# Dense projections of a two-layer encoder by token: activations stationary, 512 weight columns moving

## The chip, the cores and the metric

The kernel runs on one core of one Trainium2 chip. The metric is device time in microseconds (us) of a whole execution, median of three runs. A span in the profile runs from the first to the last instruction of one profiled execution and is a little shorter.

## The reference, cut to what matters

One sequence of 256 tokens, model width 1024, two layers, all in float32. Each layer does this (FFN width 2816, 8 query heads and 2 key heads of 64, conv width 512 with 31 taps):

```python
h = x + 0.5 * swiglu(rms_norm(x, norm_ffn1[i]), w_ffn1_in[i], w_ffn1_out[i])
u = rms_norm(h, norm_mix[i])
q, k, v, c, g = jnp.split(u @ w_in[i], splits, axis=-1)
y_attn = window_attention(q, k, v, sink[i], rel_bias) @ w_attn_out[i]
c_val, c_gate = jnp.split(c, 2, axis=-1)
c = depthwise_conv(c_val * jax.nn.sigmoid(c_gate), conv_w[i], conv_b[i])
y_conv = jax.nn.silu(layer_norm(c, conv_ln_g[i], conv_ln_b[i])) @ w_conv_out[i]
g_attn, g_conv = jnp.split(jax.nn.sigmoid(g), 2, axis=-1)
h = h + (g_attn * y_attn + g_conv * y_conv) @ w_o[i]
h = h + 0.5 * swiglu(rms_norm(h, norm_ffn2[i]), w_ffn2_in[i], w_ffn2_out[i])
x = h + (p[i] @ w_pe_proj[i]) * jax.nn.sigmoid(rms_norm(h, norm_pe[i]) @ w_pe_gate[i])
```

## The kernel before

Weights are 200 MB and are read once, in the order of use, through SyncE's queue into four 1 MB tiles called `raw`. To keep float32 accuracy, class `Weights` splits each block in two: ScalarE (ACT) casts `raw` to float32r as `w_hi` (L100), and VectorE (DVE) subtracts to get `w_lo` (L101); seven such pairs are in flight. Activations are split in the same way (`x0h`, `x0l`, `h_hi`, `h_lo`), and a product is three matmuls, high by high, high by low and low by high (`mm3`, L311 to L313).

Before, the 128x128 weight block is the stationary operand and the 256 tokens move: a matmul yields 128 features by 256 tokens in PSUM. So everything is held features on partitions: the residual `x32`, the SwiGLU layer `h`, the gates `g`. A norm's mean square is summed by GpSimd (POOL) and turned into a row that all partitions hold by a matmul with ones (`ps_stat`, L409). Only keys, values and queries (`ps_kv`, `ps_q`, L664 to L710) are made with the activation stationary. The two branch outputs `attn_out` (`ps_ao`) and `conv_out` (`ps_co`, both L837) use the raw float32 weights with no split; such a matmul leaves two records in the trace.

Each layer goes: FFN in (`ps_gu`), FFN out (`ps_fo`), then `mix`, then a second FFN, then `embed` (`ps_pp`, `ps_pe`). Inside `mix` TensorE computes conv input `ps_c`, keys, values, queries, scores `ps_s`, transposes `ps_pt`, `ps_o` and gates `ps_g`; meanwhile DVE does the convolution, 31 taps for each of four channel blocks on tile `y` (L600). Then come `ps_ao` with the conv layer norm between (mean `ps_mu` L856, variance `ps_var` L866, then `rs`, SiLU), then `ps_co`, then `ps_wo`.

A table of relative positions, `tb`, is made during the first FFN, written 128 times to DRAM as `tb_d` (2 MB from 8 partitions, L526) and read back skewed as `bias` (L530). Both transfers are issued by ACT's queue, which stands still until the first has landed before it issues the second.

A scheduler puts each engine's instructions in program order with priorities; each engine then works strictly in that order. The convolution taps have a background priority, so they fill what DVE has left.

Of the kernel before, what the change touches and what calls it, by code (L numbers as in the profile page):

```python
# [15 lines left out]
P = 128  # L16
T = 256
D = 1024
KD = D // P
L = 2  # L20
# [12 lines left out]
NEG = -1e9  # L33
LOOK = 6
# [4 lines left out]
W_BUFS = 7  # L39


class Weights:
# [16 lines left out]
    def spec(self, k, n, pieces):  # L59
        """pieces: (unit, first k of the unit, first column of the unit, first column here, columns)."""  # L60
        self.specs.append((k, n, pieces, False))

    def raw_spec(self, unit, k, c0, n):
        self.specs.append((k, n, [(unit, 0, c0, 0, n)], True))

    def limit(self):
        held = [p[0] for s in self.specs[self.next_get : self.next_prep] if s[3] for p in s[2]]
        return min(held) + RAW_BUFS - 1 if held else len(self.units) - 1

    def load_upto(self, u):  # L70
        while self.next_load <= min(u, self.limit(), len(self.units) - 1):
            k, n, sources = self.units[self.next_load]
            t = self.raw_pool.tile([P, KD * 256], F32, name="raw", tag="raw")
            v = t[:, : k * n].rearrange("p (k n) -> p k n", n=n)
            for place, src in sources:
                self.nc.sync.dma_start(place(v), src)
            self.raw[self.next_load] = v
            self.next_load += 1

    def prep_upto(self, i):  # L80
        nc = self.nc
        while self.next_prep <= min(i, len(self.specs) - 1):
            k, n, pieces, as_is = self.specs[self.next_prep]
            for u, *_ in pieces:
                self.load_upto(u + RAW_BUFS - 2)
                if u >= self.next_load:
                    return
            if as_is:
                ((u, k0, s0, _, w),) = pieces
                self.ready[self.next_prep] = self.raw[u][:, k0 : k0 + k, s0 : s0 + w]  # L90
                self.next_prep += 1
                continue
            hi = self.w_pool.tile([P, KD * P], F32R, name="w_hi")
            lo = self.w_pool.tile([P, KD * P], F32R, name="w_lo")
# [44 lines left out]
def encoder_kernel(ctx: ExitStack, tc: tile.TileContext, a: dict, out: bass.AP):  # L139
# [9 lines left out]
    mmp = ctx.enter_context(tc.tile_pool(name="mmp", bufs=4, space=PS))  # L149
    atp = ctx.enter_context(tc.tile_pool(name="atp", bufs=2, space=PS))  # L150

    def mm_tile(name):
        return mmp.tile([P, 512], F32, name=name, tag="mm")

    def at_tile(name):
        return atp.tile([P, 1024], F32, name=name, tag="at")

    # ---------------------------------------------------------------- inputs
# [3 lines left out]
    x_ld = raw_pool.tile([P, 2, D], F32, name="x_ld", tag="raw")  # L162
    xv = a["x"][0].rearrange("(t p) d -> p t d", p=P)
    for i in range(4):
        s = slice(i * 256, (i + 1) * 256)
        nc.sync.dma_start(x_ld[:, :, s], xv[:, :, s])

    col = {}
    par = const.tile([P, 96], F32, name="par")
# [13 lines left out]
    def place_params(tile_, rows, c0):  # L183
        r0 = 0
        for name in rows:
            n = 1 if name in ("q_norm", "k_norm") else a[name].shape[1] // P
            col[name] = (c0 + r0, n)
            r0 += L * n
        ps = at_tile("ps_par")
        nc.tensor.transpose(ps[:, :r0], tile_[:r0, :], ident[:r0, :r0])  # L190
        nc.scalar.copy(out=par[:, c0 : c0 + r0], in_=ps[:, :r0])
        return c0 + r0

    rows_first = const.tile([L * KD, P], F32, name="rows_first")
    load_params(rows_first, ("norm_ffn1",), nc.scalar.dma_start)

    # --------------------------------------------------------- weight stream
# [5 lines left out]
    def cols_unit(w, k, c0, n):  # L203
        return ws.unit(k, n, [(whole, w[: k * P, c0 : c0 + n].rearrange("(k p) n -> p k n", p=P))])

    def ffn_specs(w_in, w_out, quick=False):
        for j in range(KF // 2):
            if quick and j == 0:
                for c in range(2):
                    for c0 in (0, FF):  # L210
                        u = cols_unit(w_in, KD, c0 + c * P, P)
                        ws.spec(KD, P, [(u, 0, 0, 0, P)])
                continue
            ug = cols_unit(w_in, KD, j * 256, 256)
            uu = cols_unit(w_in, KD, FF + j * 256, 256)
            for c in range(2):
                ws.spec(KD, P, [(ug, 0, c * P, 0, P)])
                ws.spec(KD, P, [(uu, 0, c * P, 0, P)])
        for f in range(KD // 2):
            us = [  # L220
                ws.unit(n, 256, [(whole, w_out[k0 * P : (k0 + n) * P, f * 256 : (f + 1) * 256].rearrange("(k p) n -> p k n", p=P))])
                for k0, n in KGROUPS
            ]
            for c in range(2):
                for u, (_, n) in zip(us, KGROUPS):
                    ws.spec(n, P, [(u, 0, c * P, 0, P)])

    KGROUPS = [(0, 8), (8, 7), (15, 7)]

    def mix_specs(l):  # L230
        w = a["w_in"][l]
        c0 = QD + 2 * P

        def conv_specs(j, n):
            uv = cols_unit(w, KD, c0 + j * P, n * P)
            ug = cols_unit(w, KD, c0 + CD + j * P, n * P)
            for c in range(n):
                ws.spec(KD, P, [(uv, 0, c * P, 0, P)])
                ws.spec(KD, P, [(ug, 0, c * P, 0, P)])

        conv_specs(0, 2)
        ukv = cols_unit(w, KD, QD, 256)
        for i in range(2):
            ws.spec(KC, 256, [(ukv, i * KC, 0, 0, 256)])
        for i in range(2):
            uq = cols_unit(w[i * KC * P : (i + 1) * KC * P], KC, 0, QD)
            for k in range(0, KC, 2):
                ws.spec(2, QD, [(uq, k, 0, 0, QD)])
        conv_specs(2, 2)
        g0 = QD + 2 * P + 2 * CD  # L250
        for j in range(8):
            u = cols_unit(w, KD, g0 + j * 256, 256)
            for c in range(2):
                ws.spec(KD, P, [(u, 0, c * P, 0, P)])
        w = a["w_attn_out"][l]
        for j in range(2):
            src = w[:, j * 512 : (j + 1) * 512].rearrange("(v c p) n -> v p c n", v=2, p=HD)
            u = ws.unit(KC, 512, [
# [3 lines left out]
            for c in range(2):  # L262
                ws.raw_spec(u, KC, c * 256, 256)
        w = a["w_conv_out"][l]
        for j in range(2):
            u = cols_unit(w, KC, j * 512, 512)
            for c in range(2):
                ws.raw_spec(u, KC, c * 256, 256)
        w = a["w_o"][l]
        for j in range(4):  # L270
            u = cols_unit(w, KD, j * 256, 256)
            for c in range(2):
                ws.spec(KD, P, [(u, 0, c * P, 0, P)])

    def pe_specs(l):
        up = cols_unit(a["w_pe_proj"][l], 2, 0, 1024)
        for c in range(2):
            ws.spec(2, 512, [(up, 0, c * 512, 0, 512)])
        for j in range(4):
            u = cols_unit(a["w_pe_gate"][l], KD, j * 256, 256)  # L280
            for c in range(2):
                ws.spec(KD, P, [(u, 0, c * P, 0, P)])
# [7 lines left out]
    # ------------------------------------------------------------- constants  # L290
    ones_d = const.tile([P, P], F32, name="ones_d")
    nc.gpsimd.memset(ones_d, 1.0 / D)
# [11 lines left out]
    # -------------------------------------------------------------- helpers  # L304
    def mm3(ps, w, x, first=True, last=True, k0=0, x_k0=0, n_k=None, cols=slice(0, P)):
        (wh, wl), (xh, xl) = w, x
        n_k = wh.shape[1] if n_k is None else n_k
        for k in range(n_k):
            kx = x_k0 + k
            f, e = first and k == 0, last and k == n_k - 1  # L310
            nc.tensor.matmul(ps, wh[:, k0 + k, cols], xh[:, kx, :], start=f, stop=False)  # L311
            nc.tensor.matmul(ps, wh[:, k0 + k, cols], xl[:, kx, :], start=False, stop=False)  # L312
            nc.tensor.matmul(ps, wl[:, k0 + k, cols], xh[:, kx, :], start=False, stop=e)  # L313

    def pair(name, x, fresh):
        """Two products with x in one PSUM tile [P, 2, T]; right behind the evacuation that
        made x (fresh) its last block comes last."""
        if not fresh:
            ps = mm_tile(name).rearrange("p (c t) -> p c t", c=2)
            return ps, [lambda c=c: mm3(ps[:, c, :], ws.get(), x) for c in range(2)]  # L320
# [745 lines left out]
```

## Time and profile before

| what | value |
|---|---|
| device time, median of 3 | 1199.72 us (1199.09 to 1199.82) |
| span of the profiled execution | 1195.8 us; its own time was not kept apart, so the 3.9 us to the median stand for what lies around the span |
| TensorE (PE) matmul busy | 1160.1 us, 97% |
| DVE busy | 812.5 us, 68% |
| ACT busy | 613.9 us, 51% |
| POOL busy | 89.4 us, 7% |
| weights read by SyncE's queue | 200.01 MB |

PE waits in few places: the start, about 19 us in the first FFN, and a few us in each `mix`. In the chain of work that ended last, PE holds 91% and the transfer into `tb_d` 4%.

### The profile page before, as it was taken

How to read it: one execution, taken by the hardware profiler on the slowest of the kernel's cores; microseconds unless marked ns; L12 is line 12 of the kernel's file. 1: busy time of each engine (PE TensorE's matmuls, PEld its weight loads, DVE VectorE, ACT ScalarE, POOL GpSimd, SP SyncE). 2: the span in 40 equal slices, each digit the busy share in tenths (PEclk: the TensorE clock that was granted, in tenths of full speed). 3: DMA queues.
4: the chain of work that ended last, by engine and by line, in shares of the span. 5: the costliest groups of instructions: out<-in, count | busy, mean ns of one | idle time of the engine just before them, and what ended most of it. 6: DMA issues, size and time to landing. Idle time of an engine off the chain costs nothing.

```text
span 1195.8 us, 21809 instructions
## 1 busy us (share of the span) xinstructions
PE 1160.1 (97%) x9082; PEld 1125.0 (94%) x9082; DVE 812.5 (68%) x1214; ACT 613.9 (51%) x1033; POOL 89.4 (7%) x119
## 2 busy tenths in 40 slices
PE   7985999999999999999999999999999999999998
PEld 7985999999789999999999999999978899999997
DVE  5825765699767766665786666568986786666564
ACT  6614444477535544444674444447753564444443
POOL 3000001130001000000010000112100020000110
PEclk9996999999999999999999999999999999999999
DMA  8957645656136664555656555565531665644541
GB/s 248 288 99 209 229 151 173 215 179 152 59 105 205 193 211 158 188 180 175 200 162 210 169 179 163 194 212 177 142 106 36 213 220 175 199 154 159 194 142 36
DMA packets 196710, 205.07 MB, mean 171 GB/s; under 512 B 3731, under 2 KB 188899, under 8 KB 196612
## 3 DMA queue, kind: packets, MB, share of 16 engines
q1 hardware_dynamic: 194508, 200.01, 52.4%
q10 hardware_dynamic: 2104, 3.68, 1.9%
q8 instruction: 71, 1.16, 0.4%
q14 instruction: 27, 0.22, 0.1%
HBM read 200.53 MB, written 3.15 MB: 170 GB/s over the span
## 4 chain that ended last, share of the span: by engine, by line
PE 91%; DMA 5%; DVE 2%; ACT 1%; issue 0%; ACTq 0%
PE ps_gu L313 13%; PE ps_gu L311 13%; PE ps_gu L312 13%; PE ps_fo L312 7%; PE ps_fo L313 7%; PE ps_fo L311 7%; DMA tb_d<-tb 4%; PE ps_g L311 3%; PE ps_g L313 3%; PE ps_g L312 3%; PE ps_co L837 2%; PE ps_s L745 1%; PE ps_c L311 1%; PE ps_pe L313 1%; PE ps_pe L311 1%; PE ps_pe L312 1%
## 5 line engine op out<-in xcount | busy, mean ns | idle before, releaser
L101 DVE TENSOR_TENSOR w_lo<-raw,w_hi 128x1024 fp32r<-128x1024 f32 (+1 forms) x368 | 440.9, 1202 | 266.8 <-ACT w_hi L100 264.3
L100 ACT CAST w_hi<-raw 128x1024 fp32r<-128x1024 f32 (+1 forms) x368 | 377.4, 1030 | 443.2 <-PE ps_gu L312 196.7
L312 PE MATMUL ps_fo<-h_lo,w_hi 128*128 128x256 f32 x704 | 198.9, 283 | 0.0
L313 PE MATMUL ps_fo<-h_hi,w_lo 128*128 128x256 f32 x704 | 198.9, 283 | 0.0
L311 PE MATMUL ps_fo<-h_hi,w_hi 128*128 128x256 f32 x704 | 198.9, 283 | 0.0
L312 PEld LDWEIGHTS ps_fo<-h_lo,w_hi 128*128 128x128 f32 x704 | 135.1, 192 | 0.0
L311 PEld LDWEIGHTS ps_fo<-h_hi,w_hi 128*128 128x128 f32 x704 | 135.1, 192 | 0.0
L313 PEld LDWEIGHTS ps_fo<-h_hi,w_lo 128*128 128x128 f32 x704 | 135.1, 192 | 0.0
L400 POOL TENSOR_TENSOR sq_acc<-sq_acc,sq 128x256 f32<-128x256 f32 x56 | 56.3, 1005 | 924.7 <-ACT sq L399 924.2
L311 PE MATMUL ps_gu<-x0h,w_hi 128*128 128x256 f32 x352 | 102.6, 291 | 19.6 <-ACT w_hi L100 17.4
L313 PE MATMUL ps_gu<-x0h,w_lo 128*128 128x256 f32 x352 | 102.2, 290 | 0.7 <-DVE w_lo L101 0.7
L312 PE MATMUL ps_gu<-x0l,w_hi 128*128 128x256 f32 x352 | 101.8, 289 | 0.0
L600 DVE SCALAR_TENSOR_TENSOR y<-cpad,cw,y 128x256 f32<-128x256 f32 x240 | 101.1, 476 | 0.1
L312 PE MATMUL ps_gu<-xf1l,w_hi 128*128 128x256 f32 x352 | 100.0, 284 | 0.0
L311 PE MATMUL ps_gu<-xn0h,w_hi 128*128 128x256 f32 x352 | 100.0, 284 | 0.0
L312 PE MATMUL ps_gu<-xf0l,w_hi 128*128 128x256 f32 x352 | 99.9, 284 | 0.0
L311 PE MATMUL ps_gu<-xf1h,w_hi 128*128 128x256 f32 x352 | 99.9, 284 | 0.0
L311 PE MATMUL ps_gu<-xf0h,w_hi 128*128 128x256 f32 x352 | 99.8, 284 | 0.0
L313 PE MATMUL ps_gu<-xn0h,w_lo 128*128 128x256 f32 x352 | 99.8, 284 | 0.0
L313 PE MATMUL ps_gu<-xf1h,w_lo 128*128 128x256 f32 x352 | 99.8, 283 | 0.0
L313 PE MATMUL ps_gu<-xf0h,w_lo 128*128 128x256 f32 x352 | 99.8, 283 | 0.0
L312 PE MATMUL ps_gu<-xn0l,w_hi 128*128 128x256 f32 x352 | 99.8, 283 | 0.0
(222 smaller groups left out, 2727.9 us busy)
## 6 DMA issues: line engine op xcount, KB each, us to landing
raw<-in_w_ffn_in_dram SPq DMA_DIRECT2D x86, 1024.0 KB
raw<-in_w_in_dram SPq DMA_DIRECT2D x30, 1024.0 KB
raw<-in_w_ffn_out_dram SPq DMA_DIRECT2D x32, 896.0 KB
raw<-in_w_ffn_out_dram SPq DMA_DIRECT2D x16, 1024.0 KB
raw<-in_w_o_dram SPq DMA_DIRECT2D x8, 1024.0 KB
raw<-in_w_pe_gate_dram SPq DMA_DIRECT2D x8, 1024.0 KB
raw<-in_w_attn_out_dram SPq DMA_DIRECT2D x8, 512.0 KB
raw<-in_w_conv_out_dram SPq DMA_DIRECT2D x4, 1024.0 KB
```

Source lines behind the costliest of these rows:

```text
L100: nc.scalar.copy(out=hv[:, :, d0 : d0 + w], in_=src),
L101: nc.vector.tensor_tensor(out=lv[:, :, d0 : d0 + w], in0=src, in1=hv[:, :, d0 : d0 + w].bitcast(F32), op=ALU.subtract,),
L311: nc.tensor.matmul(ps, wh[:, k0 + k, cols], xh[:, kx, :], start=f, stop=False)
L312: nc.tensor.matmul(ps, wh[:, k0 + k, cols], xl[:, kx, :], start=False, stop=False)
L313: nc.tensor.matmul(ps, wl[:, k0 + k, cols], xh[:, kx, :], start=False, stop=e)
L400: nc.gpsimd.tensor_tensor(out=self.acc, in0=self.acc, in1=sq, op=ALU.add)
L600: nc.vector.scalar_tensor_tensor(out=y[:, i, :], in0=src, scalar=w, in1=y[:, i, :], op0=ALU.mult, op1=ALU.add)
L745: nc.tensor.matmul(ps[:, c, :], qT[v * HD : (v + 1) * HD, c, qb * P : (qb + 1) * P], kT[v * HD : (v + 1) * HD, :], start=True, stop=True,)
L837: nc.tensor.matmul(ps[:, c * T : (c + 1) * T], w[:, k, c * P : (c + 1) * P], x[:, k, :], start=k == 0, stop=k == KC - 1,)
```

## The change

It turns the dense projections around. The activation's 128 tokens by 128 features are stationary (two token blocks, `NT`), and 512 weight columns move; a matmul yields 128 tokens by 512 features (`mm3`, new L294 to L296). The function `chunk` does a whole product for 512 columns in two PSUM banks; the weight pieces change shape but not size. The residual is now `x_tok`, tokens on partitions. So a norm's gain becomes a row multiplied on DVE, its mean square an ACT accumulation, and its factor `r_x` a scalar for each partition, applied in the evacuation; no `ps_stat` any more. But the next product needs features on partitions, so each such operand goes back through PE transposes: `turn` (`ps_x`) after each norm and for the gated sum `ym`, `ps_h` for the inner layer of the FFN, `ps_ct` for the convolution's input. The final transposes of the output go away. `attn_out` and `conv_out` now use split weights and 512 columns, two chunks each in place of four pieces. Layer-norm work is now in pieces of 512 columns. The two transfers `tb_d` and `bias` are issued by POOL's queue (new L451, L455), and the gains of later norms are loaded through that queue too.

```diff
-    def mm3(ps, w, x, first=True, last=True, k0=0, x_k0=0, n_k=None, cols=slice(0, P)):
...
-            nc.tensor.matmul(ps, wh[:, k0 + k, cols], xh[:, kx, :], start=f, stop=False)
-            nc.tensor.matmul(ps, wh[:, k0 + k, cols], xl[:, kx, :], start=False, stop=False)
-            nc.tensor.matmul(ps, wl[:, k0 + k, cols], xh[:, kx, :], start=False, stop=e)
+    def mm3(ps, x, kx, t, w, k, first, last):
+        (xh, xl), (wh, wl) = x, w
+        xh, xl = xh[:, kx, tok(t)], xl[:, kx, tok(t)]
+        nc.tensor.matmul(ps, xh, wh[:, k, :], start=first, stop=False)
+        nc.tensor.matmul(ps, xh, wl[:, k, :], start=False, stop=False)
+        nc.tensor.matmul(ps, xl, wh[:, k, :], start=False, stop=last)
...
+    def turn(x, k0, t, src):
+        ps = tr_tile("ps_x").rearrange("p (f q) -> p f q", q=P)
+        for f in range(4):
+            nc.tensor.transpose(ps[:, f, :], src[:, f * P : (f + 1) * P], ident)
+        split([h[:, k0 : k0 + 4, tok(t)] for h in x], ps)
...
+        def scale(self, t, c):
+            xg = tmp.tile([P, N], F32, name="xg", tag="row", bufs=3)
+            nc.vector.tensor_tensor(out=xg, in0=x_tok[:, t, cols(c)], in1=self.gain[:, cols(c)], op=ALU.mult)
+            junk = tmp.tile([P, N], F32, name="sqj", tag="row", bufs=3)
+            nc.scalar.activation(
+                out=junk, in_=x_tok[:, t, cols(c)], func=AF.Square, scale=D ** -0.5,
+                accum_out=self.ss[:, t, c : c + 1],
+            )
+            return lambda: turn(self.x, c * KC, t, xg)
...
-        nc.scalar.dma_start(tb_d.rearrange("q h m -> h q m"), tb.unsqueeze(1).broadcast_to([NH, P, NREL]))
+        nc.gpsimd.dma_start(tb_d.rearrange("q h m -> h q m"), tb.unsqueeze(1).broadcast_to([NH, P, NREL]))
...
-        nc.scalar.dma_start(bias, skew)
+        nc.gpsimd.dma_start(bias, skew)
...
+                def turn_h():
+                    ps = tr_tile("ps_h").rearrange("p (f t) -> p f t", f=2)
+                    for f in range(2):
+                        for t in range(NT):
+                            nc.tensor.transpose(ps[:, f, tok(t)], hh[:, t, f * P : (f + 1) * P], ident)
+                    split([p[:, 2 * j : 2 * j + 2, :] for p in h], ps)
+
+                ws.later(2, turn_h)
...
-            for i in range(KC):
-                if i == 1:
-                    ln_mean()
-                if i == 2:
-                    ln_scale()
-                attn_out(2 * i)
-                if i == 0:
-                    squash(12)
...
+            attn_out(0)
+            squash(0)
+            squash(2)
+            ln_mean()
+            ws.later(2, ln_scale)
+            attn_out(1)
...
+            for c in range(2):
+                acc = acc_tile("ps_co")
+                chunk(acc, KC, yp, 2 if c else 0, after=lambda t: urgent(t, 1, acc))
```

Three places in the order of instructions matter below. The first is PE in layer 1 at the conv layer norm. Before, the last gate products are followed by `ps_ao` in four pieces with the norm's matmuls spread between them:

```order
L311 MATMUL ps_g<-xm0h,w_hi 128x256
L312 MATMUL ps_g<-xm0l,w_hi 128x256
L313 MATMUL ps_g<-xm0h,w_lo 128x256
L837 MATMUL ps_ao<-o,raw 128x256 x8
L856 MATMUL ps_mu<-y,ones_c 128x256 x2
L837 MATMUL ps_ao<-o,raw 128x256 x6
L856 MATMUL ps_mu<-y,ones_c 128x256
L837 MATMUL ps_ao<-o,raw 128x256 x2
L856 MATMUL ps_mu<-y,ones_c 128x256
L866 MATMUL ps_var<-ysq,ones_c 128x256 x2
L837 MATMUL ps_ao<-o,raw 128x256 x9
```

After, on PE at the same place, from the end of the second and last `ps_ao` chunk:

```order
L294 MATMUL ps_ao<-w_hi,o_h 128x512
L295 MATMUL ps_ao<-w_lo,o_h 128x512
L296 MATMUL ps_ao<-w_hi,o_l 128x512
L784 MATMUL ps_mu<-y,ones_c 128x256 x2
L794 MATMUL ps_var<-ysq,ones_c 128x256 x4
L294 MATMUL ps_co<-w_hi,y_h 128x512
L295 MATMUL ps_co<-w_lo,y_h 128x512
```

The second half of the mean and all of the variance now stand behind the last `ps_ao` matmul, with `ps_co` next, which needs the norm's result.

The second place is DVE at the same stage. Before, from the last gates to the norm's end:

```order
L818 TENSOR_TENSOR g<-ps_g,r_x 128x512
L600 SCALAR_TENSOR_TENSOR y<-cpad,cw,y 128x256 x12
L818 TENSOR_TENSOR g<-ps_g,r_x 128x512
L600 SCALAR_TENSOR_TENSOR y<-cpad,cw,y 128x256 x6
L847 TENSOR_TENSOR g<-ps_ao,g 128x512
L600 SCALAR_TENSOR_TENSOR y<-cpad,cw,y 128x256 x2
L847 TENSOR_TENSOR g<-ps_ao,g 128x512
L858 TENSOR_TENSOR y<-y,ps_mu 128x512 x2
L101 TENSOR_TENSOR w_lo<-raw,w_hi 128x1024 x2
L847 TENSOR_TENSOR g<-ps_ao,g 128x512
L366 RECIPROCAL rs<-sd 128x256
L870 TENSOR_TENSOR y<-y,rs 128x256 x4
```

After, on DVE, from the evacuation of the first `ps_ao` chunk (L767; taps are L538, weight splits L89):

```order
L767 TENSOR_TENSOR g<-ps_ao,g 128x512 x2
L538 SCALAR_TENSOR_TENSOR y<-cpad,cw,y 128x256 x4
L89 TENSOR_TENSOR w_lo<-raw,w_hi 128x1024
L538 SCALAR_TENSOR_TENSOR y<-cpad,cw,y 128x256 x2
L89 TENSOR_TENSOR w_lo<-raw,w_hi 128x1024
L767 TENSOR_TENSOR g<-ps_ao,g 128x512 x2
L538 SCALAR_TENSOR_TENSOR y<-cpad,cw,y 128x256
L89 TENSOR_TENSOR w_lo<-raw,w_hi 128x1024
L538 SCALAR_TENSOR_TENSOR y<-cpad,cw,y 128x256 x10
L786 TENSOR_TENSOR y<-y,ps_mu 128x512 x2
L798 RECIPROCAL rs<-sd 128x256
L801 TENSOR_TENSOR y<-y,rs 128x512 x2
```

Behind the first `ps_ao` evacuation DVE had two taps left; now it has 17, and three weight splits among them.

The third place is the queue that issues the bias table. Before, on ACT in the first FFN:

```order
L444 CAST h_hi<-hh 128x256
L100 CAST w_hi<-raw 128x1024
L526 DMA tb_d<-tb 8x128x512
L100 CAST w_hi<-raw 128x1024
L549 ACTIVATE sg<-gu 128x256
L100 CAST w_hi<-raw 128x1024
L444 CAST h_hi<-hh 128x256
L100 CAST w_hi<-raw 128x1024
L549 ACTIVATE sg<-gu 128x256
L100 CAST w_hi<-raw 128x1024
L444 CAST h_hi<-hh 128x256
L530 DMA bias<-tb_d 128x8x384
```

After, on POOL:

```order
L344 TENSOR_SCALAR nwt<-nwt 128x2
L345 TENSOR_TENSOR r_x<-r_x,nwt 128x2
L451 DMA tb_d<-tb 8x128x512
L455 DMA bias<-tb_d 128x8x384
L524 MEMSET cpad 128x4x15
L525 MEMSET cpad 128x4x15
L371 TENSOR_TENSOR ms_x<-ss 128x2
```

The transfers left ACT, and on POOL the next work behind them belongs to `mix` and to the norm at the end of the first FFN.

More of the change, by code (lines that the diff above doesn't have):

```diff
@@ L354, in group, with chunk @@
-    def group(products, evac):
-        for i, fn in enumerate(products):
-            fn()
-            if i == 0:
-                flush()
-        pending.append(evac)
-    def rsqrt_of(ps, eps, name, **kw):
-        sd = tmp.tile([P, T], F32, name="sd", bufs=1)
-        nc.scalar.activation(out=sd, in_=ps, func=AF.Sqrt, bias=eps)
-        r = tmp.tile([P, T], F32, name=name, **kw)
-        nc.vector.reciprocal(out=r, in_=sd)
-        return r
+    def chunk(acc, n_k, x, tail=0, n=N, after=None):
+        done, held = 0, []
+        while done < n_k:
+            w = ws.get()
+            k = w[0].shape[1]
+            if n_k - done <= 2 * tail:
+                held.append((w, done, k))
+            else:
+                for i in range(k):
+                    for t in range(NT):
+                        mm3(acc[:, t, :n], x, done + i, t, w, i, done + i == 0, done + i == n_k - 1)
+            if done == 0:
+                flush()
+            done += k
+        for t in range(NT):
+            for w, k0, k in held:
+                for i in range(k):
+                    mm3(acc[:, t, :n], x, k0 + i, t, w, i, k0 + i == 0, k0 + i == n_k - 1)
+            if held and after:
+                after(t)
@@ L574, in ffn @@
+                ws.later(2, turn_h)
+            chunk(acc, KD, x.x)
+            pending.append(evac)
+        for j in range(KF // 2):
             if j in hooks:
@@ L798, in gather @@
                     ov = o_ps.pop(qb).rearrange("p (c q) -> p c q", c=GROUP)
-                    nc.scalar.copy(out=o[:, :, qb * P : (qb + 1) * P], in_=ov)
+                    split([p[:, :, tok(qb)] for p in o], ov)
             for at, fn in (
@@ new lines, in squash, with attn_out @@
+            def squash(c):
+                for t in range(NT):
+                    gs = g[:, t, c * N : (c + 2) * N]
+                    tc.keep_in_program_order(nc.scalar.activation(out=gs, in_=gs, func=AF.Sigmoid))
+            for c in range(4):
+                gates(c)
+            def attn_out(c):
+                acc = acc_tile("ps_ao")
+                def evac():
+                    for t in range(NT):
+                        gs = g[:, t, cols(c)]
+                        nc.vector.tensor_tensor(out=gs, in0=acc[:, t, :], in1=gs, op=ALU.mult)
+                chunk(acc, KC, o)
+                pending.append(evac)
@@ new lines, in ln_scale @@
+                for i in range(0, KC, 2):
+                    nc.vector.tensor_tensor(out=y[:, i : i + 2, :], in0=y[:, i : i + 2, :], in1=two(rs), op=ALU.mult)
+                    for j in range(i, i + 2):
+                        nc.scalar.activation(
+                            out=y[:, j, :], in_=y[:, j, :], func=AF.Silu,
+                            scale=pcol("conv_ln_g", l, j), bias=pcol("conv_ln_b", l, j),
+                        )
+                    split([p[:, i : i + 2, :] for p in yp], y[:, i : i + 2, :])
```

768 lines of the change are left out of this document (312 added, 456 removed).

## The prediction

> **What bounds the kernel now.** I read the page's busy times and its chain first, then the waits, then PE's timeline at the shapes that the change swaps, and last the two places where PE stands still.
>
> ```profile
> span 1195.8 us, 21809 instructions
> PE 1160.1 (97%) x9082; PEld 1125.0 (94%) x9082; DVE 812.5 (68%) x1214; ACT 613.9 (51%) x1033; POOL 89.4 (7%) x119
> PE 91%; DMA 5%; DVE 2%; ACT 1%; issue 0%; ACTq 0%
> ```
>
> PE is the bound nearly everywhere: 1160 of 1196 us. So a cheaper matmul pays in full, and a new PE wait costs in full. The waits say where the other 36 us are (us in total, times, longest):
>
> ```profile
> ACT w_hi L100 <- DMA tb_d<-tb: 35.2, 1, 35.2
> PE ps_gu L311 <- ACT w_hi L100: 17.4, 1, 17.4
> PE ps_var L866 <- ACT ysq L861: 3.2, 2, 1.6
> ```
>
> ACT's casts stood behind the bias table for 35.2 us, and PE then waited 17.4 us for a cast. The layer norm holds PE only 1.6 us in each layer.
>
> **Wide matmuls.** The busy time of one matmul overlaps the next, so the price is the distance between starts. PE's timeline, first at 256 columns, then at 512 (the queries already have the activation stationary):
>
> ```profile
> 199.83 0.28 PE L312 MATMUL ps_fo<-h_lo,w_hi 128*128 128x256 f32 x1
> ...
> 203.91 0.28 PE L313 MATMUL ps_fo<-h_hi,w_lo 128*128 128x256 f32 x1
> ```
>
> ```profile
> 244.49 0.40 PE L708 MATMUL ps_q<-w_hi,xm0h 128*128 128x512 f32 x1
> ...
> 255.18 0.39 PE L710 MATMUL ps_q<-w_hi,xm0l 128*128 128x512 f32 x1
> 255.40 0.28 PE L311 MATMUL ps_c<-xm0h,w_hi 128*128 128x256 f32 x1
> ```
>
> The first pair is 34 starts apart: 4.08/34 = 0.120 us. The second is 48 matmuls from 244.49 to 255.40: 0.2273 us. Of 256 columns the kernel has 4224 (FFN in), 2112 (FFN out), 768 (gates), 384 each (conv input, w_o, embed gate) and 96 (embed projection) that change: 8352 become 4176, and each pair saves 2 x 0.120 - 0.2273 = 0.0127 us: **-53.0**.
>
> The Trainium skill speaks against that: "TensorE: Matmul & The Clock Gate", the section on 56 ns against 53.3, has warm matmuls N/2.4 GHz plus about 2.5 ns apart. By it one pair would save 2.5 ns and this term would be -10 us. This case's rows (120 ns at 256, where the rule says 109; 227 at 512, where it says 216) have a larger fixed part, about 12 ns, so I take the rows.
>
> **Branch outputs.** The raw float32 matmuls of one stage:
>
> ```profile
> 355.00 14.08 PE L837 MATMUL ps_co<-y,raw 128*128 128x256 f32 x64 [0.91 <-ACT y L871]
> 368.73 0.71 PE L311 MATMUL ps_wo<-ym_h,w_hi 128*128 128x256 f32 x3
> ```
>
> That is 13.73 us, 64 records of 0.215. After, the stage has 48 matmuls at 0.2273 = 10.91. Four such stages: **-11.3**. The eight `ps_stat` products with all tokens, two records each of that kind (0.43), go: **-3.4**.
>
> **Transposes.** PE at one existing batch:
>
> ```profile
> 415.08 0.60 PE L1003 MATMUL ps_pt<-ident,p_ld 128*128 128x128 f32 x4
> 415.44 0.36 PE L311 MATMUL ps_gu<-xf0h,w_hi 128*128 128x256 f32 x1
> 415.64 0.28 PE L312 MATMUL ps_gu<-xf0l,w_hi 128*128 128x256 f32 x1
> ```
>
> Four transposes end 0.36 us later, and the next matmul takes 0.20 instead of 0.12: 0.11 each. Added: 7 norms x 16, FFN inner layers 44 x 4, conv inputs 16, `ym` 32; taken away: 16 at the output; the 16 of the input stay. Net 320 x 0.11 = **+35.2**. PE's own work so changes by -53.0 - 11.3 - 3.4 + 35.2 = **-32.5**. The casts and subtractions behind the transposes replace evacuations of like size on ACT and DVE, both well under PE; they cost nothing as long as PE has other products queued, which it has in the FFNs.
>
> **The bias table.** The chain, PE's last cold stretch, and the DMA queues from 60 to 104 us (q10 is the bias table's, q1 the weights'):
>
> ```profile
> 55.82 44.68 DMA tb_d<-tb
> 100.52 0.40 ACTq L530
> 101.01 1.05 ACT w_hi L100
> 102.09 1.24 DVE w_lo L101
> ```
>
> ```profile
> 85.00:90.00 5.00, 0.00 (x0) 0.00 (x0) 0.00 (x0) 0.00 (x0) 0.00 (x0) 0.79 0.50 71
> 100.00:105.00 5.00, 2.43 (x9) 2.13 (x10) 2.91 (x4) 3.62 (x5) 0.00 (x0) 0.50 0.85 290
> 105.00:110.00 5.00, 5.00 (x32) 5.00 (x31) 4.99 (x8) 3.29 (x7) 0.00 (x0) 0.67 0.73 248
> ```
>
> ```profile
> q10 hardware_dynamic: 1349, 2.57, 45.0%
> q1 hardware_dynamic: 2086, 2.10, 14.3%
> ```
>
> (Columns of the middle fence: window, length, busy time of PE, its weight loads, DVE, ACT, POOL, then granted clock, DMA share, GB/s.) The share stands at 0.50 at 71 GB/s while the table is written: half of the 16 engines are busy, as 8 source partitions suggest, and a weight load, which needs all 16, crawls with it. So two things held PE: ACT stood behind the transfer, and the weights starved. The change removes the first. I estimate that 2 MB of landed weights then can still be cast, four pieces of 24 matmuls at 0.120 = 11.5 us of PE work, and PE stops some 6.5 us instead of 18: **-11.5**. The ends are 0 (weights starve just as long) and -20 (no stop, no cold clock). On POOL the `bias` issue waits about 45 us behind `tb_d`; behind it stand pads and the norm that ends the first FFN, some 100 us later, so it hides; if POOL stood until then, that norm would be late by the excess.
>
> **Start and end.** The first gain row (512 KB on all partitions) and 16 transposes come ahead of the first product: +1 (0 to 3). At the end the multiplication by `r`, the last transposes and their copy go: -2 (0 to -2.5), by the rows
>
> ```profile
> 1189.02 0.43 DVE L960 TENSOR_TENSOR sg<-ps_pe,r_x 128x256 f32<-128x256 f32 x1 [1.22 <-PE ps_pe L313]
> 1191.02 0.41 PE L975 MATMUL ps_out<-ident,x 128*128 128x128 f32 x2 [1.60 <-DVE x L964]
> 1192.14 0.37 ACT L977 COPY ot<-ps_out 128x256 f32<-128x256 f32 x1 [0.82 <-DMA out_dram<-ot]
> ```
>
> **The layer norm.** This is the largest loss. Durations at that stage (count, busy, mean ns; the first row is 16 taps in 6.42 us, 0.40 each):
>
> ```profile
> 319.12 6.42 DVE L600 SCALAR_TENSOR_TENSOR y<-cpad,cw,y 128x256 f32<-128x256 f32 x16
> ```
>
> ```profile
> L101 DVE TENSOR_TENSOR w_lo<-raw,w_hi 128x1024 fp32r<-128x1024 f32 x7 | 8.3, 1222 | 8.5 <-ACT w_hi L100 8.5
> L100 ACT CAST w_hi<-raw 128x1024 fp32r<-128x1024 f32 x7 | 7.0, 1044 | 7.2 <-DMA raw<-in_w_o_dram 7.2
> L847 DVE TENSOR_TENSOR g<-ps_ao,g 128x512 f32<-128x512 f32 x4 | 2.8, 688 | 3.4 <-PE ps_ao L837 3.4
> L871 ACT ACTIVATE y<-y,par 128x256 f32<-128x256 f32 x4 | 2.2, 592 | 1.2 <-DVE y L870 1.2
> L366 DVE RECIPROCAL rs<-sd 128x256 f32<-128x256 f32 x1 | 1.7, 1744 | 0.0
> L364 ACT ACT_TABLE_LOAD x1 | 1.3, 1283 | 0.0
> L861 ACT ACTIVATE ysq<-y 128x512 f32<-128x512 f32 x2 | 1.2, 630 | 7.7 <-DVE y L858 7.7
> L824 ACT ACTIVATE g<-g 128x1024 f32<-128x1024 f32 x1 | 1.1, 1057 | 6.1 <-DVE g L818 6.1
> ```
>
> I walk the new order from the last matmul of the first `ps_ao` chunk. PE has 21 matmuls left, 4.8 us. DVE waits for two gate sigmoids behind a table load on ACT (done at 1.7), then does two products (2.4), four taps (4.0), a weight split whose cast ends at 4.9 behind two more sigmoids (6.1), two taps (6.9), a split (8.1), two products (9.4), a tap, a split (11.0) and ten taps (15.0). PE waits 15.0 - 4.8 = 10.2 us. From there nothing covers the norm: mean 0.9, subtraction 1.3, square 0.6, variance 0.9, table load and root 1.8, reciprocal 1.7, product 0.7, four SiLU 2.2 and a cast 0.6: 10 us with 2.6 of it PE's, so 7.4 idle. Both together 17.6, less the 0.91 and 1.61 of before: +15 in each layer, **+30**. The clock: its mean is 0.79 over the first window of the long stop, so it falls some 3 us after PE stops, and 0.67 from 105 to 110, so it is half until about 108, 4.9 us after the restart, worth 2.4. Either new wait is longer than 3 us; with the half-speed norm matmuls between them about 4 in each layer: **+8** (0 to 10).
>
> **Other joints in `mix`.** In the attention, PE's new order puts score transposes and `ps_o` right behind one another with no gate product between. Three places wait for a copy or scaling of the size of the cast above (1.04), 0.5 to 1.6 each; `ps_co` to w_o (product, sum, transposes, split, partly covered) about 2, and w_o to the next FFN about 1. No row shows these; the nearest is the 1.6 of `ps_var`. 6.5 in each layer, **+13** (0 to 26).
>
> **The sum.** 1195.8 - 32.5 - 11.5 + 1 - 2 + 30 + 8 + 13 = 1201.8 us of span, plus the 3.9 that the median has over the span: **1206**, its own range 1195 to 1217. It is slower by 0.5%; 0.2% (2.4 us) is what can be told from no change.
>
> **Rivals.** *The bias table costs nothing any more.* If the weights no longer starve, the 6.5 us and 2.4 of cold clock go too: 1197, just faster. For it: the table is made 20 us earlier in the program, and POOL's queue may spread it otherwise. Against it: the share of 0.50. The Trainium skill ("DMA: Bandwidth & Descriptors", on how many engines a DMA uses) takes the number of engines from the slowest dimension, 8 here, for either kind of queue; by that the starving stays and so does my term.
>
> *The norm is covered after all.* If DVE reaches the last tap before PE ends the second `ps_ao` chunk, the 10.2 us of each layer and half of its cold clock go, 24 us: 1182, faster by 1.5%. It decides at one point: the last tap within 4.8 us of the first chunk's end. Before, DVE had two taps left there; the order with 17 speaks against it. Half of all waits in `mix` gives about the same time.
>
> *POOL's queue is slower.* If it moves the table at half the pace, PE stops as long as before or longer: 18 more than my sum, 1224. No row shows this queue with a large transfer.
>
> *The wide matmul gains 2.5 ns a pair*, the rule above: 1206 + 43 = 1249. The rows at both widths speak against it.
>
> **How the numbers follow.** The sum as worked: 0.50 (faster 0.06, same 0.12, slower 0.32 within its range). Bias table free: 0.14 (faster 0.09, same 0.05). Norm covered: 0.20, faster. Slow queue: 0.14, slower. Narrow gain: 0.02, slower. That makes 0.35 faster, 0.17 same, 0.48 slower. The range 1178 to 1222 takes in the covered norm at 1182 and leaves out its lower part and the upper part of the slow queue.
>
> **What would show it.** In the profile after: 0.227 us between starts in the FFN and four transposes in 0.44; PE's waits led by `ps_mu` for `y` (about 20 us in two) and `ps_co` for `y_h` (about 13); a stop of about 6.5 us in the first FFN, with ACT not behind `tb_d`. I am wrong if PE's wait at `ps_mu` is short, if the stop is gone or as long as before, or if FFN matmuls lie further apart.

## The result and the profile after

The changed kernel takes 1237.91 us (1235.83 to 1238.64) against 1199.40 for the kernel before on the same chip: ratio 1.0321, 95% interval 1.0306 to 1.0335. It is slower, as forecast, but by 38.5 us and not by 6. The page after:

```profile
span 1235.9 us, 13683 instructions
PE 1155.6 (94%) x5137; PEld 924.3 (75%) x5137; DVE 736.4 (60%) x1008; ACT 627.6 (51%) x967; POOL 55.7 (5%) x127
PE 81%; DVE 8%; ACT 6%; DMA 3%; issue 1%; POOL 0%; SPq 0%; DVEq 0%; ACTq 0%
```

PE's instructions fell by 43%, its busy time only by 4.5 us, and PE stands idle 80 us, 45 more than before. What PE waited for (us in total, times, longest):

```profile
PE ps_mu L784 <- DVE y L538: 18.1, 2, 9.0
PE ps_h L478 <- DVE hh L470: 17.2, 1, 17.2
PE ps_co L294 <- ACT y_h L329: 11.4, 2, 5.7
PE ps_pe L294 <- ACT sge L872: 8.4, 3, 4.9
PE ps_x L336 <- DVE xg L361: 7.4, 1, 7.4
```

The first and third rows are the layer norm's, which the prediction had walked through. The second is the stop at the bias table: it has kept its length, though ACT no longer stands behind the transfer. The fourth, in the embedding step, the prediction did not have. The last is the start of the kernel.

The first fence shows the layer norm on PE's timeline in layer 1. In brackets stand the idle time ahead of a row and what ended it; before the change these were 1.61 us at `ps_var` and 0.91 us at `ps_co`. The second fence shows the same stage by windows (length, then busy time of PE, its weight loads, DVE, ACT and POOL, then granted clock, DMA share, GB/s):

```profile
352.77 2.08 PE L784 MATMUL ps_mu<-y,ones_c 128*128 128x256 f32 x4 [9.04 <-DVE y L538]
356.28 3.78 PE L794 MATMUL ps_var<-ysq,ones_c 128*128 128x256 f32 x8 [1.44 <-ACT ysq L789]
365.75 0.79 PE L294 MATMUL ps_co<-w_hi,y_h 128*128 128x512 f32 x1 [5.69 <-ACT y_h L329]
```

```profile
346.00:355.00 9.00, 2.08 (x4) 1.18 (x4) 7.23 (x16) 0.00 (x0) 0.00 (x0) 0.52 0.37 117
355.00:360.00 5.00, 3.72 (x8) 2.52 (x8) 1.16 (x2) 2.51 (x3) 0.00 (x0) 0.50 0.00 0
366.00:371.00 5.00, 5.00 (x14) 3.90 (x15) 1.03 (x2) 0.22 (x1) 0.00 (x0) 0.58 0.00 0
371.00:376.00 5.00, 5.00 (x23) 4.04 (x22) 1.90 (x3) 1.73 (x2) 0.00 (x0) 1.00 0.22 57
```

The idle times 9.0, 1.4 and 5.7 make 16.2 us. The variance runs at a granted clock of 0.50, and the first `ps_co` matmuls are slow too: the window from 366 has 14 matmuls at a mean clock of 0.58, the next one 23 at 1.00. The bias table's stop by windows, where PE now works until 102 us:

```profile
95.00:100.00 5.00, 5.00 (x23) 4.13 (x22) 0.00 (x0) 0.00 (x0) 0.00 (x0) 1.00 0.49 59
100.00:105.00 5.00, 2.43 (x11) 1.69 (x9) 0.00 (x0) 0.00 (x0) 0.00 (x0) 1.00 0.67 103
115.00:120.00 5.00, 0.32 (x2) 0.32 (x3) 4.86 (x6) 4.23 (x7) 0.00 (x0) 0.50 1.02 360
```

While the table is written, the DMA share is about half, as before, at 59 GB/s, and DVE and ACT have nothing to split. As soon as weights land again both are nearly full (4.86 and 4.23 of 5 us; of the 360 GB/s there, a part is the table that is read back).

The span grew by 40.1 us. To place them I added up, for each kind of product, the distances from each matmul's start to the next one's in the two traces, so that a wait counts for the product ahead of it. The predicted terms stand beside the sums:

| stage (us) | before | after | change | predicted |
|---|---|---|---|---|
| FFN in, with its transposes, without the stop | 514.0 | 506.4 | -7.6 | -7.4 |
| the stop in the first FFN | 17.7 | 17.6 | 0 | -11.5 |
| FFN out and w_o | 299.2 | 294.4 | -4.8 | -15.8 |
| conv input, keys, values, queries, gates | 176.2 | 168.4 | -7.8 | -7.3 |
| embedding (`ps_pp`, `ps_pe`) | 58.3 | 68.9 | +10.6 | -3.0 |
| branch outputs and layer norm, cold clock | 68.0 | 97.5 | +29.5 | +26.7 |
| attention (predicted: all joints of `mix`) | 40.2 | 45.0 | +4.8 | +13.0 |
| transposes for norms, `ym`, conv; output and `ps_stat` gone | 11.8 | 23.6 | +11.8 | +12.4 |
| start, end and rest | 10.4 | 13.9 | +3.5 | -1.0 |

Three rows hold the miss: the stop (11.5), FFN out with w_o (11.0) and the embedding (13.6). For FFN out the reason is mostly the price of one matmul. PE's timeline, first in `ps_gu` (FFN in), then in `ps_up` (FFN out and w_o):

```profile
465.70 0.39 PE L295 MATMUL ps_gu<-w_lo,xf0h 128*128 128x512 f32 x1
...
469.78 0.39 PE L295 MATMUL ps_gu<-w_lo,xf0h 128*128 128x512 f32 x1
```

```profile
209.84 0.39 PE L294 MATMUL ps_up<-w_hi,hh 128*128 128x512 f32 x1
...
218.43 0.39 PE L295 MATMUL ps_up<-w_lo,hh 128*128 128x512 f32 x1
```

In `ps_gu` 18 steps take 4.08 us, 0.2267 each; in `ps_up` 37 steps take 8.59 us, 0.2322 each. Over all of `ps_up` the mean is 0.2346, without the two longest waits.

### The profile page after: what moved, and what is told of

Read it like the earlier page. It is cut to its first block, busy times and chain, and to the rows that moved or that the text cites. A ratio compares the mean times of both kernels' runs of the same rounds, so it can differ in the third digit from the quotient of the medians.

```text
span 1235.9 us, 13683 instructions
## 1 busy us (share of the span) xinstructions
PE 1155.6 (94%) x5137; PEld 924.3 (75%) x5137; DVE 736.4 (60%) x1008; ACT 627.6 (51%) x967; POOL 55.7 (5%) x127
## 4 chain that ended last, share of the span: by engine, by line
PE 81%; DVE 8%; ACT 6%; DMA 3%; issue 1%; POOL 0%; SPq 0%; DVEq 0%; ACTq 0%
PE ps_gu L296 12%; PE ps_gu L294 12%; PE ps_gu L295 12%; PE ps_up L296 8%; PE ps_up L294 8%; PE ps_up L295 8%; DMA raw<-in_w_ffn_in_dram 3%; DVE w_lo L89 3%; DVE y L538 2%; PE ps_h L478 2%; ACT w_hi L88 2%; PE ps_o L721 1%; PE ps_pe L294 1%; PE ps_g L294 1%; PE ps_pe L296 1%
## 5 line engine op out<-in xcount | busy, mean ns | idle before, releaser
L89 DVE TENSOR_TENSOR w_lo<-raw,w_hi 128x1024 fp32r<-128x1024 f32 x376 | 458.8, 1223 | 391.5 <-ACT w_hi L88 390.6
L88 ACT CAST w_hi<-raw 128x1024 fp32r<-128x1024 f32 x376 | 393.9, 1051 | 436.3 <-PE ps_gu L296 175.6
L296 PE MATMUL ps_up<-w_hi,hl 128*128 128x512 f32 x352 | 139.6, 397 | 0.0
L295 PE MATMUL ps_up<-w_lo,hh 128*128 128x512 f32 x352 | 139.6, 397 | 0.0
L294 PE MATMUL ps_up<-w_hi,hh 128*128 128x512 f32 x352 | 138.9, 395 | 0.0
L538 DVE SCALAR_TENSOR_TENSOR y<-cpad,cw,y 128x256 f32<-128x256 f32 x240 | 100.4, 476 | 0.0
L294 PEld LDWEIGHTS ps_up<-w_hi,hh 128*128 128x128 f32 x352 | 66.3, 188 | 15.4
L296 PEld LDWEIGHTS ps_up<-w_hi,hl 128*128 128x128 f32 x352 | 66.2, 188 | 15.4
L296 PE MATMUL ps_gu<-w_hi,x0l 128*128 128x512 f32 x176 | 71.2, 405 | 0.1
L295 PE MATMUL ps_gu<-w_lo,x0h 128*128 128x512 f32 x176 | 70.9, 403 | 0.0
L294 PE MATMUL ps_gu<-w_hi,x0h 128*128 128x512 f32 x176 | 70.7, 402 | 0.0
L295 PE MATMUL ps_gu<-w_lo,xf1h 128*128 128x512 f32 x176 | 69.7, 397 | 0.0
L295 PE MATMUL ps_gu<-w_lo,xf0h 128*128 128x512 f32 x176 | 69.7, 397 | 0.0
L296 PE MATMUL ps_gu<-w_hi,xn0l 128*128 128x512 f32 x176 | 69.4, 395 | 0.0
L294 PE MATMUL ps_gu<-w_hi,xf0h 128*128 128x512 f32 x176 | 68.8, 392 | 0.2 <-ACT xf0h L329 0.2
L294 PE MATMUL ps_gu<-w_hi,xf1h 128*128 128x512 f32 x176 | 68.8, 392 | 0.2 <-ACT xf1h L329 0.2
L294 PE MATMUL ps_gu<-w_hi,xn0h 128*128 128x512 f32 x176 | 69.0, 392 | 0.0
L296 PE MATMUL ps_gu<-w_hi,xf1l 128*128 128x512 f32 x176 | 68.7, 394 | 0.0
L296 PE MATMUL ps_gu<-w_hi,xf0l 128*128 128x512 f32 x176 | 68.7, 394 | 0.0
L478 PE MATMUL ps_h<-ident,hh 128*128 128x128 f32 x176 | 33.7, 273 | 17.2 <-DVE hh L470 17.2
```

The costliest lines, as they stand in the source:

```text
L88: nc.scalar.copy(out=hv[:, :, d0 : d0 + w], in_=src),
L89: nc.vector.tensor_tensor(out=lv[:, :, d0 : d0 + w], in0=src, in1=hv[:, :, d0 : d0 + w].bitcast(F32), op=ALU.subtract,),
L294: nc.tensor.matmul(ps, xh, wh[:, k, :], start=first, stop=False)
L295: nc.tensor.matmul(ps, xh, wl[:, k, :], start=False, stop=False)
L296: nc.tensor.matmul(ps, xl, wh[:, k, :], start=False, stop=last)
L478: nc.tensor.transpose(ps[:, f, tok(t)], hh[:, t, f * P : (f + 1) * P], ident)
```

## The experiments

All runs on the changed kernel are compared with its 1237.91 us. The kernel before took 1198.4 to 1199.7 us on the chips of these runs, so a difference of about 1 us means nothing. Theory E says that the bias table's write holds the DMA engines, theory D that at the layer norm PE waits for a late DVE; the other letters are explained in the expectations.

**The queue alone.** Both transfers back on ACT's queue in the changed kernel, and on POOL's in the kernel before:

```diff
-        nc.gpsimd.dma_start(tb_d.rearrange("q h m -> h q m"), tb.unsqueeze(1).broadcast_to([NH, P, NREL]))
+        nc.scalar.dma_start(tb_d.rearrange("q h m -> h q m"), tb.unsqueeze(1).broadcast_to([NH, P, NREL]))
...
-        nc.gpsimd.dma_start(bias, skew)
+        nc.scalar.dma_start(bias, skew)
```

> The changed kernel, with only the two bias-table transfers back on ACT's queue. Theory E (the table's write holds half the DMA engines, and weights starve whoever issues it): within 4 us of the changed kernel's 1238, PE's stop in the first FFN stays 14 to 21 us. Rival Q (what counts is which queue stands still): ACT stops casting again, the stop grows by the predicted 11.5 us, 1249. Rival S (POOL's queue starves the weights harder than ACT's): 5 to 10 us faster, 1228 to 1233.

> The kernel before, with only the two bias-table transfers moved to POOL's queue. Theory E: within 4 us of 1199, PE's stop stays near 18 us. Rival Q, which the prediction rested on: the stop falls from 18 to 6.5 us, 1188. Rival S: 5 to 10 us slower, 1204 to 1209.

Measured: 1245.97 and 1188.66 us, that is 8.1 slower than the changed kernel and 9.8 faster than the kernel before. PE's wait at the stop in the two, changed kernel first:

```profile
PE ps_h L478 <- DVE hh L470: 26.9, 1, 26.9
```

```profile
PE ps_gu L311 <- ACT w_hi L100: 8.5, 1, 8.5
```

So rival Q holds in the main: the queue shortens the stop from 17.4 to 8.5 us in one kernel and from 26.9 to 17.2 in the other, some 9 us where the prediction had 11.5. Theory E's claim that the queue makes no difference falls. But on one and the same queue the wide kernel stops about 9 us longer.

**The table through all engines.** The 16 KB table goes to DRAM once, and is copied there 128 times:

```diff
-        nc.gpsimd.dma_start(tb_d.rearrange("q h m -> h q m"), tb.unsqueeze(1).broadcast_to([NH, P, NREL]))
+        nc.gpsimd.dma_start(tb_1, tb)
+        nc.gpsimd.dma_start(tb_d, tb_1.unsqueeze(0).broadcast_to([P, NH, NREL]))
```

> The changed kernel, where the 16 KB table goes to DRAM once and is then copied 128 times from DRAM to DRAM, queries as the slowest dimension, still by POOL's queue, so that all 16 DMA engines can share it. Theory E: the write takes 15 us or less, no weight load waits long, PE's stop of 17 us goes and with it 2.4 us of half clock: 1218. Rivals Q and S (the queue counts, not the engines): the stop stays, 1234 to 1240.

> The kernel before with the same DRAM to DRAM copy on POOL's queue. Theory E: PE's stop of 18 us and 2.4 us of half clock go, 1179. Rivals Q and S: 1188 to 1209, as for the queue alone.

Measured: 1218.30 and 1176.94 us (ratio of the latter to the kernel before 0.9819, interval 0.9804 to 0.9833). POOL's timeline in the former:

```profile
70.30 0.57 POOL L453 DMA_DIRECT2D tb_d<-tb  x1 [2.58 <-DMA tb<-tb]
79.97 0.94 POOL L457 DMA_DIRECT2D bias<-tb_d  x1 [9.09 <-DMA tb_d<-tb]
```

The copy took under 10 us in place of 44.7, and no stop is left in either trace. So the length of the write matters, as E said, and the queue beside it, as Q said. In the changed kernel the DMA share is 0.75 and 0.84 in the windows from 70 to 80 us, where it was about 0.50 during the old write. But the copy also reads DRAM in place of 8 partitions of SBUF, and the runs do not part that from the number of engines. The kernel before with this copy beats both kernels. Without any stop the rest of the change costs 41 us.

**Why the stop is longer in the wide kernel.** In the changed kernel's trace, 32 weight pieces had both parts ready when PE stopped, and PE had done 368 matmuls on them, which is 30.7 pieces: 16 matmuls, 3.6 us, were ready and not begun. PE stood at the transposes `ps_h`; these wait for `hh`, which DVE makes, and DVE stood at the low part of a weight that had not landed. Such a wait behind the head of a queue is called head-of-line blocking. The test leaves the inner layer's transposes out (the second product then gets operands in the wrong layout, of the right shape):

```diff
-                    ps = tr_tile("ps_h").rearrange("p (f t) -> p f t", f=2)
-                    for f in range(2):
-                        for t in range(NT):
-                            nc.tensor.transpose(ps[:, f, tok(t)], hh[:, t, f * P : (f + 1) * P], ident)
-                    split([p[:, 2 * j : 2 * j + 2, :] for p in h], ps)
+                    split([p[:, 2 * j : 2 * j + 2, :] for p in h], hh)
```

> The changed kernel without the 176 PE transposes of the FFN's inner layer: the two halves h_h and h_l are split straight from the untransposed tile, so the FFN's second product has wrong operands of the right shape. Theory T: each transpose is worth 0.11 us of PE, 19.4 us in all. Theory H (in the bias table's stop, PE stood with 16 ready matmuls behind a transpose, whose input waited on DVE behind a split of starved weights): the stop falls from 17.6 to about 9 us, so 1238 - 19.4 - 8.5 = 1210. Rival W (the stop is only the weights' late landing): it stays at 17, 1218.

Measured: 1212.88 us, 25 less. Its wait for the stop:

```profile
PE ps_gu L294 <- ACT w_hi L88: 11.7, 1, 11.7
```

FFN in without the stop adds up to 486.6 in place of 506.4: 19.8 us for 176 transposes, 0.11 each, as predicted. The stop falls by 5.5, with all 32 pieces used. So of the 8.7 us that the wide kernel stops longer on POOL's queue, the run shows 5.5 to be this head-of-line wait. The other 3.2 can be read off two traces with the table on POOL's queue, the old kernel's and this one's, though no run tests it. After the write was issued, PE worked on for 39.9 us in the old kernel (331 matmuls of 0.12) and for 36.0 here (158 of 0.2267), that is 13.8 and 13.2 pieces; it had weights again 48.4 and 47.8 us after the issue. A faster PE is through much the same stock sooner, and then stands longer.

**The layer norm.** 12 of 31 taps left out (the output of the convolution is then another):

```diff
-                        for t in range(TAPS):
+                        for t in range(TAPS - 12):
```

> The changed kernel with 12 of the 31 convolution taps left out in each channel block, about 19 us less DVE work in each layer. Theory D (at the layer norm PE waits for a DVE that has not finished its taps): PE's wait at ps_mu falls from 18.1 to under 2 us in all, the wait at ps_co stays near 11, and the time falls by 18 to 24 us, to 1214 to 1220. Rival C (the norm's own chain behind the last ps_ao sets it, the taps only fill the time): the wait moves from ps_mu to ps_var and ps_co, less than 8 us gained.

Measured: 1216.30 us, 21.6 less. `ps_mu` left the list of waits, and `ps_co` moved little:

```profile
PE ps_co L294 <- ACT y_h L329: 13.7, 2, 6.9
```

Theory D holds: the first wait is DVE's lag. The second has stayed without that lag, so it belongs to the norm's own chain.

**Taking DVE work away without leaving any out.** The low parts of the branch-output weights on POOL, first for both branches, then for `conv_out` alone and with the table's copy:

```diff
-                    nc.vector.tensor_tensor(
+                    (nc.gpsimd if pool else nc.vector).tensor_tensor(
```

> The changed kernel, where the low parts of the two branch-output weights (8 pieces in each layer, 1.2 us each on DVE) are made on POOL. Theory D: nearly 10 us of DVE work in each layer leaves the stretch in which the taps lag, PE's wait at ps_mu falls from 18.1 to 2 us or less, 14 to 20 us faster, 1218 to 1224. Rival P (POOL is slower at this than the time it has, by its 1.0 us for 128x256 about 4 us a piece, and slows DVE beside it): PE waits for w_lo in ps_ao instead, 1234 or more.

> The changed kernel with the DRAM to DRAM table copy and with only conv_out's low weight parts (4 pieces in each layer) made on POOL. By theories E and D: 19.6 us from the table as measured, and 5 us less DVE work in each layer ahead of the last tap, with the second half of the attention result no longer behind 31 taps: PE's waits at ps_mu and ps_ao together fall from 18 to about 8 us, 1238 - 19.6 - 10 = 1208. If POOL beside DVE slows DVE, 1215 or more. Not faster than the kernel before by either.

Measured: 1228.58 us, 9.3 less and not 14 to 20; and 1217.63, which is 0.7 under the copy alone, no more than chips differ, and not 10. In the former `ps_mu` no longer waits, but 31 taps now stood ahead of the attention result's low part on DVE, and PE waited 10.4 us for that; and the taps became longer. PE's wait there, and the groups of instructions in `mix` of layer 1 (count, busy, mean ns):

```profile
PE ps_ao L296 <- DVE o_l L330: 10.4, 2, 5.2
```

```profile
L538 DVE SCALAR_TENSOR_TENSOR y<-cpad,cw,y 128x256 f32<-128x256 f32 x120 | 64.4, 606 | 0.0
L89 POOL TENSOR_TENSOR w_lo<-raw,w_hi 128x1024 fp32r<-128x1024 f32 x8 | 23.3, 2914 | 14.9 <-ACT w_hi L88 12.5 <-DVE y L538 2.3
```

The same with `conv_out` alone on POOL, and its waits at `ps_mu`:

```profile
L540 DVE SCALAR_TENSOR_TENSOR y<-cpad,cw,y 128x256 f32<-128x256 f32 x120 | 56.9, 538 | 0.0
L89 POOL TENSOR_TENSOR w_lo<-raw,w_hi 128x1024 fp32r<-128x1024 f32 x4 | 10.1, 2531 | 18.3 <-ACT w_hi L88 18.3
```

```profile
PE ps_mu L786 <- DVE y L540: 15.0, 4, 6.0
```

And the taps in the changed kernel:

```profile
L538 DVE SCALAR_TENSOR_TENSOR y<-cpad,cw,y 128x256 f32<-128x256 f32 x120 | 50.2, 477 | 0.0
```

With eight splits on POOL the 120 taps keep DVE busy 14.2 us longer, and those splits had cost DVE 9.8; with four it is 6.7 against 4.9. So rival P's second half is right: POOL took more of DVE's time than it gave back. That the former kernel is faster all the same comes from the places of the waits: 18.1 less at `ps_mu`, 10.4 more at `ps_ao`.

The mean of 606 ns hides two kinds of taps. On DVE and POOL at one of the eight subtractions:

```profile
318.36 3.02 DVE L538 SCALAR_TENSOR_TENSOR y<-cpad,cw,y 128x256 f32<-128x256 f32 x2
318.58 2.51 POOL L89 TENSOR_TENSOR w_lo<-raw,w_hi 128x1024 fp32r<-128x1024 f32 x1 [2.01 <-ACT w_hi L88]
```

The two taps take 3.02 us because the second, begun after POOL's subtraction, lasts until it is over. In each of seven of the eight subtractions one tap so takes 2.55 to 2.63 us, and the other 113 taps keep 0.48 on average. The eighth subtraction itself takes 5.57 us, while taps run on. On these operands the two engines took turns by whole instructions.

**The embedding.** Two kernels. The first only frees an accumulator (the first three added lines), the second also changes the order:

```diff
+            pps = [tmp.tile([P, N], F32, name=f"pps{t}", tag="hh") for t in range(NT)]
+            for t in range(NT):
+                nc.scalar.copy(out=pps[t], in_=pp[:, t, :])
...
-            chunk(acc, KD, st.x, 4 if c else 0, after=lambda t: urgent(t, pp, acc))
+            chunk(acc, KD, st.x, 2 if c else 0, after=lambda t: urgent(t, pp, acc))
...
-                    ws.later(3, lambda: [turns.pop(0)() for _ in range(2)])
+                    ws.later(4, lambda: [turns.pop(0)() for _ in range(2)])
```

> The changed kernel, where the embedding projection ps_pp is copied out of PSUM by ACT at once (two copies of 128x512 each time). Theory B (in the embedding step PE waits for an accumulator: ps_pp and ps_pe of the first half hold two of the three until the norm's factor is there): PE's wait at ps_pe for sge, 8.4 us, goes, 7 to 9 us faster, 1229 to 1231. Rival N (the wait is for the norm's factor, whoever holds the buffer): the same wait at the next evacuation, under 2 us gained.

> The changed kernel with ps_pp copied out of PSUM as before, and in the embedding step's second half only the last four of eight feature blocks held back (before all eight were), with the transposes of the first half's result one weight piece later. Theory F (the first half's evacuation, some 7 us of table load, sigmoids, products, sums and gain products, had only ps_pp of the second half as cover, because every other matmul of that half stood behind a taken accumulator or behind the transposes): PE's waits at ps_pe for sge and at ps_x for xg, 8.4 and 7.4 us with the start's 7.2, fall to the start's 7.2 and less than 5 more; 5 to 9 us faster, 1229 to 1233. Rival N (the norm's factor is late, not the cover short): the waits stay above 8, within 2 us of 1238.

Measured: 1237.00 and 1233.28 us. With only the accumulator free, 0.9 us is gained, no more than chips differ: PE waited for the next thing of the same evacuation, `xg` for the transposes (12.6 with the start's 7.2):

```profile
PE ps_x L336 <- DVE xg L361: 12.6, 2, 7.2
```

So theory B falls as a cause by itself. With the order changed too, 4.6 us are gained where theory F expected 5 to 9, and 6.7 us of these waits are left where it expected less than 5: F is borne out in part. The chain that PE had too little other work to cover is seen on ACT in the changed kernel:

```profile
615.99 1.28 ACT L872 ACT_TABLE_LOAD   x1 [1.76 <-PE ps_pe L296]
617.28 0.69 ACT L872 ACTIVATE sge<-ps_pe,r_x 128x512 f32<-128x512 f32 x1
617.87 1.03 ACT L88 CAST w_hi<-raw 128x1024 fp32r<-128x1024 f32 x1
...
620.08 0.67 ACT L872 ACTIVATE sge<-ps_pe,r_x 128x512 f32<-128x512 f32 x1
```

and on PE:

```profile
620.80 0.79 PE L294 MATMUL ps_pe<-w_hi,xeh 128*128 128x512 f32 x1 [4.90 <-ACT sge L872]
```

The first sigmoid stands behind a table load of 1.28 us, the second behind a weight cast and a norm's square; only then does PE's next `ps_pe` start, after 4.9 us of idle time.

**The gaps between wide matmuls.** One kernel shifts the activations in memory (one weight pair less ahead of them, and a pad; the trace shows no addresses), one changes the order within a product:

```diff
         nc.tensor.matmul(ps, xh, wh[:, k, :], start=first, stop=False)
-        nc.tensor.matmul(ps, xh, wl[:, k, :], start=False, stop=False)
-        nc.tensor.matmul(ps, xl, wh[:, k, :], start=False, stop=last)
+        nc.tensor.matmul(ps, xl, wh[:, k, :], start=False, stop=False)
+        nc.tensor.matmul(ps, xh, wl[:, k, :], start=False, stop=last)
```

> The changed kernel with six weight pairs in flight and not seven, and a 256-byte pad ahead of the FFN's inner layer, so that all activations lie elsewhere in memory. In question is why 512-column matmuls are 0.2345 us apart on average in ps_up and 0.2267 in the steady part of ps_gu. Theory A (where the stationary operand lies): the repeating pattern of gaps in ps_up (229 and 237 ns by turns) changes, to near 227 or otherwise. Rival O (the order of instructions): the same pattern as before. The one pair less may cost some us of waits.

> The changed kernel with the three matmuls of a product in another order: high by high, low by high, high by low, so that the stationary operand changes at each and the moving one repeats once. In question is the larger gap in ps_up (0.2345 on average, patterns of seven and of two matmuls) against 0.2267 in ps_gu. If the pattern comes from which operand is loaded next, it changes in ps_up, perhaps to 0.227, worth up to 9 us; if it is set by the transposes and waits ahead of a stage, ps_up stays above 0.23.

One execution each: 1245.22 and 1238.13 us. The former also stops longer at the bias table, 22.5 us, with one weight pair less. In both, `ps_up` keeps a mean above 0.234 and the same two patterns in FFN out, one of two steps (229 and 237 or 238 ns) and one of seven (228 to 241); `ps_gu` keeps 226, 227, 227. The pattern changes from one to the other right behind a group of transposes and then stays, in all four FFNs alike. Even the queries `ps_q`, from which the prediction took 0.2273, are 0.2330 apart on average in the changed kernel. The shift that was tried and the order within a product are not the cause; what sets the pattern is open.

## Why the prediction was right or wrong

The sign was right, and for the reason given as the largest loss: PE waited 18.1 us at `ps_mu` and 11.4 at `ps_co`, where I had walked about 20 and 13, and the whole stage came to +29.5 against +26.7. The wide matmul's gain in `ps_gu` and the 0.11 us of a transpose were sized well. The sum for the projections in `mix` came out too, but partly by luck: a gate matmul was 0.125 us before and 0.235 after, both above the rows that I had used, and the two errors cancel. The joints of `mix` were too dear. Three steps failed.

*The bias table, -11.5.* The four extra weight pieces were right to the piece: 24 used before the stop and 28 with POOL's queue in the old kernel, 28 and 32 ready in the new one (26.7 and 30.7 used). What failed is taking the old kernel's stop as the base to subtract from. In the new kernel with the old queue the stop was 26.9 us and not 17.4, so with POOL's queue 17.2 were left and not 6.5. Of these 10.7 us, 2.0 are the queue's gain, taken too large even for the old kernel (8.5 left there); 5.5 are DVE's starved weight split, which the transposes put in PE's way; and 3.2 are the stock that lasts PE less long, read off the traces and not tested. A stop as long as before was named as a sign of being wrong, and it came true. The rival of a slow POOL queue was not needed for this: the write took 45.4 us on it against 44.7. Nor was the table made 20 us earlier, as the first rival had it: its write was issued at 67.5 us, 11.7 later than before.

*The wide price, 0.2273 everywhere.* I took it from one product of 48 matmuls and gave no range. `ps_up` needs 0.2346 with its short waits: 1248 matmuls at 7 ns more are 9 of the 11 us in that row. Why the steps are longer there stays open.

*The embedding, no row.* I added up the joints of `mix` and walked through none outside it. The embedding got only the matmul's gain of 3 us, and the row came to +10.6; PE's waits for `sge` alone are 8.4. Freeing the accumulator and changing the order brought back 4.6.

The range, 1178 to 1222, was too narrow above because these three add up in one direction, and the last two were in no case and no rival.

## What to carry to other kernels

Here, turning a product gained only the fixed part of a matmul, about 13 ns in 240, and paid for every operand that must be turned back; count both before the waits. A transpose that feeds the next product ties PE to whatever stands ahead of its source on another engine, so a stall of that engine reaches PE with work still ready. Where the engine that sets the time has less other work to hide a chain behind, walk through every stage with such a chain, also those that the change hardly touches.

## What the runs showed of the hardware that I had not expected

POOL beside DVE slowed DVE's taps from 477 to 606 ns on average with eight subtractions and to 538 with four, and did so by holding single taps for a whole subtraction, about 2.6 us, and not by slowing all. The same 2 MB table took 44.7 us to write from 8 partitions and under 10 us to copy from DRAM, with the queries as the slowest dimension. Equal wide matmuls run in patterns, 226.7, 232.4 or 233.5 ns apart on average, which change behind transposes and hold until the next ones.
